# mLSTM of a two-layer diffusion backbone: masked attention over all keys replaced by 128-token blocks with carried states, and the projections interleaved with the blocks

## The chip, the core and the metric

The kernel runs on one core of a Trainium2 chip. A core has TensorE (PE, matmuls, with PEld loading its weights), VectorE (DVE), ScalarE (ACT), GpSimd (POOL) and SyncE (SP), each with an instruction queue of its own that it works through in order. ScalarE, GpSimd and SyncE also issue DMA transfers from their queues. The metric is the device time of one execution in microseconds.

## The reference, cut to what matters

512 latent tokens and 256 context tokens, width 1024, go through two layers. Layer 0 is a mixer and a convolutional FFN; layer 1 is latent attention and an FFN. The change touches layer 0's mixer only. It projects the normed tokens to a gated convolution branch (`a`, `g`), to `q`, `k`, `v`, an output gate `o` and 16 gate columns, runs a 31-tap depthwise convolution on the first branch and an mLSTM in both directions on the rest, and multiplies both, side by side, by `w_out`:

```python
def step(carry, inp):
...
    c_mat, n_vec, m = carry
    b = jnp.cumsum(lf, axis=-1)
    log_d = jnp.where(lower, b[..., :, None] - b[..., None, :] + li[..., None, :], -jnp.inf)
    log_inter = b + m[..., None]
    m_row = jnp.maximum(log_inter, jnp.max(log_d, axis=-1))
    s = jnp.einsum('bhid,bhjd->bhij', qj, kj) * jnp.exp(log_d - m_row[..., None])
    inter = jnp.exp(log_inter - m_row)
    num = jnp.einsum('bhij,bhjv->bhiv', s, vj) + inter[..., None] * jnp.einsum('bhvd,bhid->bhiv', c_mat, qj)
    den = jnp.sum(s, axis=-1) + inter * jnp.einsum('bhd,bhid->bhi', n_vec, qj)
    h = num / jnp.maximum(jnp.abs(den), jnp.exp(-m_row))[..., None]
...
h_ctx_seq, st_f, st_b = scans(ctx, zero, zero)
h_lat_seq, _, _ = scans(lat, st_f, st_b)
...
u = jax.nn.silu(_layer_norm(_dwconv(a * jax.nn.sigmoid(g), conv_w, conv_b), ln_g, ln_b))
hm = _rms(h_seq) * head_gain * jax.nn.sigmoid(o)
y = jnp.concatenate([u, hm], axis=-1) @ w_out
```

4 heads, keys of 64, values of 128. The forward scan runs over the context and then the latent tokens, the backward scan over each of them reversed. What chunk length is used does not change the result, and neither does computing the whole as masked attention over all earlier keys.

## The kernel before, in words

Tokens lie on the free axis in six tiles of 128 (0 to 3 latent, 4 and 5 context), channels on the partitions. A projection (`proj`, L160) splits weights and activations into two `fp32r` halves and sums three products: weight halves `wh` (ScalarE, L156) and `wl` (a subtraction, on GpSimd in the mixer, L157), the raw load `wr` on SP. An output tile of 128 channels is 48 matmuls of 384 columns. Each engine works in the order in which the scheduler lays its instructions; weights are given a priority that lifts them ahead of their place in the program.

`mixer0` (L507) goes through these steps:
- load, modulation, and the four GLU tiles (`pa`, `pg`, L569 to L593). Each gives an `up`, and 30 taps on VectorE (`conv_taps`, L560) that are taken up in small portions by `step` while later projections run.
- gate columns (`gwh`/`gwl`, `pgt`), then `gates` (L699): the log gates, prefix sums and running maxima (scans, L736 to L743), and for each of six blocks a row of decays `rr`, written to DRAM as table `rd` from ScalarE's queue (L782 to L787).
- `v` (L681) and `q`/`k` (L667), both kept as two `fp32r` halves; the output gate `so`, a tanh (L614).
- `mlstm` (L842 on): 12 units of a head and a pair of query tiles. For each unit the scores over all keys (`pqk`, three products each), broadcast loads of `rd` rows into `rf` and `rb`, masks on GpSimd, exponents, products with the scores and row sums on VectorE, transposes of the result (`pt`, split to `pth`/`ptl`), and the product with `v` (`phm`). A string `PAT0` sets in which order a unit's parts, the layer norm of the conv branch (`layer_norm`, L791, generator `L`), the rest of the ada modulations (`ada_pe`, L290, `U`, with weight loads `wa` through the `wr` buffers) and the `early` part of `w_out` (`pea`, `E`) stand.
- the product with `w_out` (`pab`, L632 to L649), residual, and the row sums for the next norm; then the FFN.

## Time and profile before

| | us |
|---|---|
| median of 3 runs (lowest, highest) | 1813.59 (1813.35, 1816.11) |
| the profiled execution | 1809.91 |
| its span | 1807.8 |
| TensorE busy in the span | 1722.2 (95%), 9614 instructions |
| TensorE weight loads | 1547.6 (86%) |
| VectorE busy | 1185.6 (66%), 1957 instructions |
| ScalarE busy | 707.5 (39%) |
| GpSimd busy | 251.4 (14%) |
| chain that ended last, by engine | PE 79%, DVE 11%, DMA 3%, ACT 3% |

The mean granted clock of TensorE is 0.957 of full speed. The two FFNs and layer 1 take the larger part of the span, from 485 us on. The mixer of layer 0 lies between 64 us (the end of the loads and of the first GLU tile) and 485 us: projections and conv taps to 254, the mLSTM with the layer norm to 416, `w_out` to 485. Row names: `out<-in` gives the tiles, a line of a helper (L103, L106, L109, L112) stands for any instruction that goes through it, and `<-` behind idle time names what ended it.

### The profile page before, as it was taken

The numbers are of one execution on the slowest core, as the hardware profiler recorded it, in microseconds if no ns is written. First come the engines' busy times: TensorE is split into PE (matmuls) and PEld (weight loads), VectorE is DVE, ScalarE is ACT, GpSimd is POOL, SyncE is SP. The second block draws the span as 40 slices with busy tenths as digits, with TensorE's granted clock in tenths as the row PEclk, the third lists the DMA queues.
The fourth block names the chain that finished last, engine by engine and source line by source line (L and its number), as shares of the span: only waits on it lengthen the run. The fifth ranks groups of instructions, "written<-read, shape, count | busy, mean of one in ns | idle before, by whom it ended". The sixth has DMA issues, their size and how long they took to land.

```text
span 1807.8 us, 24942 instructions
## 1 busy us (share of the span) xinstructions
PE 1722.2 (95%) x9614; PEld 1547.6 (86%) x9614; DVE 1185.6 (66%) x1957; ACT 707.5 (39%) x1352; POOL 251.4 (14%) x346
## 2 busy tenths in 40 slices
PE   6969887999999999999999999899999899999998
PEld 3968875669899999999999879899988788888887
DVE  4798987768694646364334487778788854444453
ACT  4212236642342121212222345787776442332232
POOL 2324223314300000000000111233140200000000
PEclk8989997779999999999999999999999899999999
DMA  9311135546252436263121241101110133333322
GB/s 345 103 37 47 47 114 170 172 150 184 77 151 82 140 99 194 70 198 92 61 59 59 80 111 53 39 13 36 34 44 24 36 94 101 98 94 97 102 90 73
DMA packets 201638, 174.78 MB, mean 97 GB/s; under 512 B 9288, under 2 KB 175606, under 8 KB 201520
## 3 DMA queue, kind: packets, MB, share of 16 engines
q1 hardware_dynamic: 198848, 169.60, 30.7%
q0 software_dynamic: 1216, 3.34, 0.5%
q8 instruction: 76, 1.25, 0.3%
q10 hardware_dynamic: 1456, 0.25, 0.1%
q14 instruction: 42, 0.34, 0.1%
HBM read 167.83 MB, written 5.33 MB: 96 GB/s over the span
## 4 chain that ended last, share of the span: by engine, by line
PE 79%; DVE 11%; DMA 3%; ACT 3%; issue 2%; POOL 1%; SPq 0%; POOLq 0%; ACTq 0%; DVEq 0%
PE pfo L103 16%; PE pfg L103 16%; PE pfv L103 16%; DVE acc L564 6%; PE psc L103 3%; PE pab L103 3%; PE ppv L103 2%; PE pt L1354 2%; PE pmo L103 2%; PE puq L103 2%; PE pukv L103 2%; PE pf L103 2%; PE pqk L103 1%; PE pcq L103 1%; PE phm L103 1%
## 5 line engine op out<-in xcount | busy, mean ns | idle before, releaser
L106 ACT ACTIVATE wh<-wr 128x1024 fp32r<-128x1024 f32 (+3 forms) x205 | 204.5, 999 | 608.6 <-PE pfo L103 220.4
L157 DVE TENSOR_TENSOR wl<-wr,wh 128x1024 fp32r<-128x1024 f32 (+3 forms) x171 | 195.6, 1146 | 195.4 <-ACT wh L106 191.4
L103 PE MATMUL pfo<-hh,wh 128*128 128x384 f32 (+2 forms) x528 | 167.2, 356 | 0.0
L103 PE MATMUL pfo<-hl,wh 128*128 128x384 f32 (+2 forms) x528 | 166.5, 354 | 0.0
L103 PE MATMUL pfo<-hh,wl 128*128 128x384 f32 (+2 forms) x528 | 166.2, 354 | 0.0
L112 DVE SCALAR_TENSOR_TENSOR xr<-pfo,mods,xr 128x512 f32<-128x512 f32 (+1 forms) x128 | 83.7, 664 | 105.5 <-PE pfo L103 104.9
L103 PE MATMUL pfg<-fh,wh 128*128 128x384 f32 (+1 forms) x504 | 151.9, 355 | 0.0
L103 PE MATMUL pfg<-fl,wh 128*128 128x384 f32 (+1 forms) x504 | 151.4, 354 | 0.0
L103 PE MATMUL pfg<-fh,wl 128*128 128x384 f32 (+1 forms) x504 | 151.1, 353 | 0.0
L103 PE MATMUL pfv<-fh,wh 128*128 128x384 f32 (+1 forms) x504 | 150.6, 352 | 0.0
L103 PE MATMUL pfv<-fh,wl 128*128 128x384 f32 (+1 forms) x504 | 150.6, 352 | 0.0
L103 PE MATMUL pfv<-fl,wh 128*128 128x384 f32 (+1 forms) x504 | 150.6, 352 | 0.0
L564 DVE SCALAR_TENSOR_TENSOR acc<-up,par,acc 128x783 f32<-128x783 f32 x120 | 135.4, 1165 | 1.9 <-ACT acc L106 1.1
L157 POOL TENSOR_TENSOR wl<-wr,wh 128x1024 fp32r<-128x1024 f32 (+1 forms) x34 | 93.1, 2740 | 252.3 <-ACT wh L106 234.2
L112 DVE SCALAR_TENSOR_TENSOR ga<-gr,cc,ga 128x1024 f32<-128x1024 f32 (+1 forms) x84 | 99.7, 1215 | 24.4 <-DMA gr<-in_ada_w_dram 24.3
L235 POOL TENSOR_TENSOR ss<-ss,sq 128x256 f32<-128x256 f32 (+1 forms) x31 | 32.6, 1057 | 583.1 <-ACT sq L106 581.5
L109 DVE TENSOR_TENSOR ft<-ft,pfv 128x768 f32<-128x768 f32 (+1 forms) x42 | 34.4, 820 | 109.9 <-PE pfv L103 109.9
L103 PEld LDWEIGHTS pfo<-hl,wh 128*128 128x128 f32 x528 | 98.1, 189 | 8.8 <-issue 0.2
L103 PEld LDWEIGHTS pfo<-hh,wh 128*128 128x128 f32 x528 | 97.8, 189 | 9.0 <-ACT hh L106 0.4
L103 PEld LDWEIGHTS pfo<-hh,wl 128*128 128x128 f32 x528 | 97.9, 189 | 8.8
L103 PEld LDWEIGHTS pfg<-fl,wh 128*128 128x128 f32 x504 | 92.8, 189 | 6.5
L103 PEld LDWEIGHTS pfg<-fh,wh 128*128 128x128 f32 x504 | 92.6, 189 | 6.6
(410 smaller groups left out, 3929.4 us busy)
## 6 DMA issues: line engine op xcount, KB each, us to landing
wr<-in_ffn_w_in_dram SPq DMA_DIRECT2D x88, 512.0 KB
gr<-in_ada_w_dram SPq DMA_DIRECT2D x48, 512.0 KB
wr<-in_ffn_w_out_dram SPq DMA_DIRECT2D x32, 512.0 KB
wa<-in_ada_w_dram SPq DMA_DIRECT2D x24, 512.0 KB
wr<-in_ab_w_in_dram SPq DMA_DIRECT2D x20, 512.0 KB
wr<-in_ffn_w_out_dram SPq DMA_DIRECT2D x24, 384.0 KB
wa<-in_ada_w_dram SPq DMA_DIRECT2D x8, 1024.0 KB
gr<-in_ada_w_dram SPq DMA_DIRECT2D x16, 256.0 KB
```

The lines of the kernel that those rows point to most:

```text
L103: self.nc.tensor.matmul(out, lhsT=lhsT, rhs=rhs, start=start, stop=stop)
L106: self.nc.scalar.activation(out, in_, func, **kw)
L109: self.nc.vector.tensor_tensor(out, a, b, op=op)
L112: self.nc.vector.scalar_tensor_tensor(out, a, s, b, op0=op0, op1=op1, **kw)
L157: self.lo_eng.tensor_tensor(lo[:, :n], raw[:, :n], hi[:, :n].bitcast(F32), op=ALU.subtract)
L235: eng.tensor_tensor(self.ss[:, s:e], self.ss[:, s:e], sq[:, s:e], op=ALU.add)
L564: nc.vector.scalar_tensor_tensor(acc[:, :CONVO], up[:, k:k + CONVO], self.convw[:, 4 * k + ct:4 * k + ct + 1], acc[:, :CONVO], op0=ALU.mul ...
L1354: nc.tensor.transpose(pt[:, o:o + P], pe[:, (j + jj) * P:(j + jj + 1) * P], self.ident)
```

## The change

The blocks carry a state per head, `C` (64 by 128 values and, through a column of ones beside `v`, the normaliser: 129 columns). `update` transposes a block of `k`, weighs it with `wc`, multiplies it with `v1` and adds the decayed old state. Five backward states `cb` are computed ahead, in the order 5, 4, 3, 2, 1; the forward state `cf` goes on with each block. A block takes scores of its own 128 keys alone (`pst`), the exponents `ex` (from table `ad`, loaded on SP, masked on GpSimd), and the carried part `ib` (table `qd`, multiplied with `q` on GpSimd); `pn` sums both for each direction, its last column is `den`. All of these products are plain float32. No broadcast rows `rf`/`rb`, no halves of `q`, `k` or `v`, no transposed probabilities. `finish` norms two blocks and multiplies them into `so`.

```diff
+PAT0 = 'c' + 'mtttt' * 3 + 'c' + 'mttttt' * 2 + 'ctttt' + 'mttttt' + 'c' + 'omtttttt' * 4 + 'F' + 'mmallmall' * 6
+MH = 3
-EM = 2
+MLSTM = {"S": (2, 2), "M": (2, 2)}
...
             gg = self.gates(pgt, gsm, slot)
             next(gg)
-            vt = self.vproj(win, hs, slot)
-            self.qkproj(win, hs, qk := [])
+            q, k = self.qkproj(win, hs)
+            for _ in glu(1):
+                self.step(TAP)
+            v1 = self.vproj(win, hs)
             G = next(gg)
...
+            gens = {"c": [glu(2), glu(3)], "o": [gate_o()], "a": [mods()], "m": [cell], "l": [ln]}
+            for o in PAT0:
+                if o == "t":
+                    self.step(1)
+                elif o == "F":
+                    self.flush()
+                else:
+                    run(o)
...
+            for m in range(MH):
+                w = self.weights(wout, 0, 4, m * P, P)
+                pss.append(self.psum_even("pab"))
+                self.proj(pss[m], w, 0, ins, 4, both, last=False)
...
+        for i, r in enumerate((f, b)):
+            nc.scalar.dma_start(ad[i].rearrange("t h n -> h t n"), blocks(a)[r])
...
+        for i in range(2):
+            for h in range(4):
+                r = 32 * i + h
+                nc.scalar.dma_start(dd[i, h // 2, h % 2:h % 2 + 1], dec[r:r + 1])
+                nc.scalar.dma_start(qd[:, h % 2, i, h // 2:h // 2 + 1].rearrange("t o n -> o t n"), blocks(ir)[r:r + 1])
+        for i in range(2):
+            for h in range(4):
+                nc.scalar.dma_start(dcol[64 * (h % 2):64 * (h % 2) + 64, 2 * i + h // 2],
+                                    dd[i, h // 2, h % 2:h % 2 + 1].partition_broadcast(64))
...
+        def update(i, t, old, new):
+            ps = self.pt("M", "pu")
+            for pr in range(2):
+                nc.tensor.transpose(ps[:, pr * P:(pr + 1) * P], k[pr][:, bl(t)], self.ident)
+            kw = mp.tile([P, 4, 64], F32, tag="kw", bufs=1, name=self.name("kw"))
+            self.tt(kw, ps[:, :256].rearrange("p (h c) -> p h c", h=4),
+                    wc[:, t, i].unsqueeze(2).to_broadcast([P, 4, 64]), ALU.mult)
+            for pr, o in ((0, 512), (1, 0)):
+                self.mm(ps[:, o:o + W2], kw[:, 2 * pr:2 * pr + 2, :].rearrange("p h c -> p (h c)"), v1(pr, t), True, True)
...
+            ex = [mp.tile([P, 4, P], F32, tag="ex", bufs=3, name=self.name("ex")) for _ in range(2)]
...
+                for h in range(4):
+                    self.act(ex[i][:, h], ex[i][:, h], AF.Exp, bias=cc[:, t, i, h:h + 1])
+            ib = mp.tile([P, 2, 2, P], F32, tag="ib", bufs=2, name=self.name("ib"))
...
+                        if st is not None:
+                            self.mm(pn[:, o + b * VW:][:, :VW], ib[:, i, pr], st[:, b * VW:(b + 1) * VW], True, False)
+                        self.mm(pn[:, o + b * VW:][:, :VW], ex[i][:, 2 * pr + b], v1(pr, t)[:, b * VW:(b + 1) * VW], st is None, True)
```

In `PAT0`, `c` is half a GLU tile (2 and 3), `o` one output gate, `t` one conv tap, `m` one part of `mlstm` (an update, or a third of a block), `a` half of an ada modulation, `l` a piece of the layer norm, `F` what is left of the taps. The order of the projections becomes GLU0, gates, q/k, GLU1, v, and then this string; `early` is gone, and the upper half of three `w_out` tiles (`MH`) stands behind the mLSTM instead.

Three places show how the instructions move. The first is GpSimd's queue ahead of the weights of GLU1's second half: `wl_1036` is the low half of GLU1's first, `wl_1090` that of its second; `ex` and `ib` are the exponents and carried parts of the first two blocks. As changed:

```order
L165 TENSOR_TENSOR wl_1036<-wr_1034,wh_1035 128x1024
L982 AFFINE_SELECT ex_1655<-ex_1655 128x512
L982 AFFINE_SELECT ex_1656<-ex_1656 128x512
L982 AFFINE_SELECT ex_1985<-ex_1985 128x512
L745 MEMSET v_139_1151 128x6
...
L991 TENSOR_TENSOR ib_1673<-ib_1673,qk_845 128x2x128
L991 TENSOR_TENSOR ib_1673<-ib_1673,qk_973 128x2x128
L991 TENSOR_TENSOR ib_2003<-ib_2003,qk_845 128x2x128
L991 TENSOR_TENSOR ib_2003<-ib_2003,qk_973 128x2x128
L165 TENSOR_TENSOR wl_1090<-wr_1088,wh_1089 128x1024
```

Three masks and four products of the mLSTM stand between the two weight halves. Before, GLU1 had both of its halves early, and the gate scans' initial values alone stood between later ones:

```order
L157 TENSOR_TENSOR wl_1242<-wr_1240,wh_1241 128x1024
L728 MEMSET mk_1115 36x768
...
L157 TENSOR_TENSOR wl_1292<-wr_1290,wh_1291 128x1024
L733 MEMSET m_1119 36x768
L734 MEMSET pf_1120 36x768
L157 TENSOR_TENSOR wl_1374<-wr_1372,wh_1373 128x1024
L772 MEMSET rr_1667 36x768
L157 TENSOR_TENSOR wl_1446<-wr_1444,wh_1445 128x1024
```

The second place is ScalarE's queue at the same point, as changed; `fg` and `z` are gate rows, `wh_1089` is the high half of GLU1's second weights. The 16 issues to `dd` and `qd` alternate, two rows of them stand here:

```order
L831 DMA ad<-fg_705 4x6x128 x2
L111 ACT_TABLE_LOAD
L111 ACTIVATE dec<-dec 36x6
L111 ACTIVATE qk_973<-pqk_924 128x768
L111 ACTIVATE z_716<-z_716 36x768
L849 DMA dd<-dec 1x6
L850 DMA qd<-z_716 6x1x128
...
L853 DMA dcol<-dd 64x6 x8
L111 ACTIVATE qk_1030<-pqk_981 128x768
L111 ACTIVATE wh_1089<-wr_1088 128x1024
```

Before, the table's issues came between the projections of `so`; here the weights behind the gates' last activation follow at once:

```order
L106 ACTIVATE fg_1097<-pgt_1037 36x768
L106 ACTIVATE e_1103<-fg_1097 36x768
L106 ACTIVATE e_1103<-e_1103 36x768
L106 ACT_TABLE_LOAD
L106 ACTIVATE z_1108<-w_1106 36x768
L106 ACTIVATE wh_1291<-wr_1290 128x1024
L106 ACTIVATE wh_1373<-wr_1372 128x1024
L106 ACTIVATE wh_1445<-wr_1444 128x1024
```

So the 26 issues, each of which waits for its gate row, stand ahead of a weight half that GLU1 needs.

The third place is TensorE in the last part of the mLSTM: `pada` the ada products, `pu` an update, `pst` the scores of a block, `pn` its sums. As changed:

```order
L108 MATMUL pada_2464<-wa_2467,cc_107 32x512 x2
L108 MATMUL pr_2486<-ss,sel 6x128 x5
L936 MATMUL pu_2516<-ident,qk_910 128x128
L936 MATMUL pu_2516<-ident,qk_1030 128x128
L108 MATMUL pada_2464<-wa_2473,cc_107 32x512 x2
L108 MATMUL pu_2516<-v_139_1151,kw_2519 128x258
L108 MATMUL pst_2581<-qk_845,qk_910 128x128 x2
L108 MATMUL pst_2581<-qk_973,qk_1030 128x128 x2
L108 MATMUL pada_2464<-wa_2475,cc_107 32x512 x2
L108 MATMUL pu_2516<-v_141_1153,kw_2519 128x258
L108 MATMUL pn_2590<-cf,ib_2576 128x129
L108 MATMUL pn_2590<-v_139_1151,ex_2558 128x129
```

Before, at the like place, a unit's products and transposes stood between them:

```order
L103 MATMUL pac_2867<-selq,arow_2802 128x2 x4
L103 MATMUL pr_2826<-hsq_2578,sel 6x128 x4
L103 MATMUL pada_2873<-wa_2874,cc_107 32x512 x2
L103 MATMUL pada_2873<-wa_2943,cc_107 32x512 x2
L103 MATMUL phm_2949<-pth_2858,vh_1344 128x256
L103 MATMUL phm_2949<-ptl_2859,vh_1344 128x256
L103 MATMUL phm_2949<-pth_2858,vl_1345 128x256
```

The ada products now stand between one block's update and the next block's scores and sums.

## Rows read from the trace of the kernel before

**Rows 1.** windows of the span: us, busy of each engine (instructions), granted clock, DMA share, GB/s

```profile
64.00:254.00 190.00, 167.47 (x882) 158.09 (x880) 181.21 (x201) 40.65 (x58) 60.29 (x34) 0.94 0.17 48
254.00:416.00 162.00, 144.06 (x716) 98.69 (x716) 116.73 (x370) 91.13 (x181) 41.38 (x71) 0.78 0.55 173
...
485.00:1808.00 1323.00, 1298.59 (x7376) 1193.28 (x7376) 806.34 (x1228) 530.26 (x1034) 99.29 (x192) 0.98 0.28 83
```

**Rows 2.** chain of waits, 64 to 300 us: start, length, what

```profile
75.23 3.07 DVE acc L564
...
92.92 15.48 DVE acc L564 x14
...
132.04 9.52 PE pgt L103 x44
141.57 4.54 PE pv L103 x20
...
162.79 3.94 DVE pf L736
...
175.87 0.95 DVE c L109
...
252.08 1.56 DMA rd<-rr
253.79 2.88 DMA rf<-rd
```

**Rows 3.** tile `acc`, the conv taps: duration ns min/median/max, first and last start

```profile
L564 DVE SCALAR_TENSOR_TENSOR acc<-up,par,acc x120: 1012/1022/3185, 71.0 to 248.8; 128x783 f32<-128x783 f32 x120
```

**Rows 4.** groups of instructions by shape, VectorE, 254 to 416 us: busy, mean ns

```profile
L109 DVE TENSOR_TENSOR ptl<-pt,pth 128x512 fp32r<-128x512 f32 x28 | 18.7, 677 | 6.7 <-ACT pth L106 6.7
...
L112 DVE SCALAR_TENSOR_TENSOR rf<-rb,dr,rf 128x128 f32<-128x128 f32 x20 | 7.2, 360 | 9.2 <-ACT rf L106 9.0
...
L112 DVE SCALAR_TENSOR_TENSOR dr<-den,dr 128x2 f32<-128x2 f32 x24 | 5.9, 244 | 0.1
...
L112 DVE SCALAR_TENSOR_TENSOR acc<-th,acc 128x768 f32<-128x768 f32 x4 | 3.8, 945 | 0.0
```

**Rows 5.** the same view, ScalarE, 64 to 416 us

```profile
L106 ACT ACTIVATE wh<-wr 128x1024 fp32r<-128x1024 f32 x17 | 18.0, 1057 | 74.2 <-PE pqk L103 14.9 <-PE pv L103 14.7 <-issue 9.3
...
L106 ACT ACTIVATE rf<-rf,acol 128x128 f32<-128x128 f32 x8 | 3.2, 394 | 4.8 <-POOL rf L873 4.8
```

**Rows 6.** tile `pm`, the one product of plain float32 over wide columns

```profile
L103 PE MATMUL pm<-s,ones x4: 379/486/697, 272.9 to 274.1; 128*128 128x512 f32 x2, 128*128 128x256 f32 x2
```

**Rows 7.** waits, 64 to 254 us: who for whom, total us, times, longest

```profile
ACT so L106 <- DMA rd<-rr: 12.4, 1, 12.4
...
PE pgt L103 <- DVE gwl L109: 10.9, 1, 10.9
```

**Rows 8.** chain of waits, 250 to 490 us

```profile
341.37 4.96 DMA wa<-in_ada_w_dram
...
416.75 33.83 PE pab L103 x192
...
484.87 1.22 PE pf L103 x2
```

**Rows 9.** tile `rd`, one kind of DMA issue on ScalarE's queue: ns min/median/max

```profile
L787 ACTq DMA_DIRECT2D rd<-rr x6: 247/250/253, 216.7 to 252.1; - x6
```

**Rows 10.** groups by shape, GpSimd, 64 to 485 us

```profile
L873 POOL TENSOR_SCALAR_AFFINE_SELECT rf<-rf 128x128 f32<-128x128 f32 x24 | 8.8, 371 | 43.0 <-DMA rf<-rd 42.5 <-PE pada L103 0.4
...
L235 POOL TENSOR_TENSOR ss<-ss,sq 128x256 f32<-128x256 f32 x6 | 5.8, 968 | 0.0
```

**Rows 11.** timeline of GpSimd, 74 to 97 us: start, length, what

```profile
74.25 3.21 POOL L157 TENSOR_TENSOR wl<-wr,wh 128x1024 fp32r<-128x1024 f32 x1 [5.00 <-ACT wh L106]
```

**Rows 12.** DMA issues, 254 to 416 us, the ada weights

```profile
wa<-in_ada_w_dram SPq DMA_DIRECT2D x21, 512.0 KB
```

More of the change, by code (lines that the diff above doesn't have):

```diff
@@ L467, in load_x @@
         nc = self.nc
-        xs = [self.xp.tile([P, T], F32, tag="x", name=f"x{k}") for k in range(KD)]
+        xs = [self.xtile(f"x{k}") for k in range(KD)]
         def src(t, c0, c1):
@@ L568, in mixer0, with glu @@
             accs = []
-            for ct in range(4):
+            def glu(ct):
                 if ct == 0:
@@ new lines, in mixer0 @@
+            hm = []
+            for h in range(4):
+                hi = ob.tile([P, T], F32R, name=self.name("hmh"))
+                gain = self.hgain[:, h:h + 1]
+                self.act(hi, so[:, h], AF.Copy, scale=gain)
+                lo = ob.tile([P, T], F32R, name=self.name("hml"))
+                self.stt(lo, so[:, h], gain, hi.bitcast(F32), ALU.mult, ALU.subtract)
+                hm.append((hi, lo))
+            xs = []
+            for k in range(KD):
+                xs.append(self.xtile(f"xr{k}"))
@@ L665, in gate_weights, with qkproj @@
         return gwh, gwl
-    def qkproj(self, win, hs, qk):
-        qk.extend([None] * 4)
+    def qkproj(self, win, hs):
+        out = [None] * 4
         for m in (0, 2, 1, 3):
@@ L687, in vproj, with gates @@
                               c == 0, c == 3, 2 * c)
[L688 to L699 removed]
+            self.step(TAP)
+        for t in range(NT):
+            for pr in range(2):
+                src = pst[t // 2][:, t % 2 * 512 + pr * 256:][:, :256].rearrange("p (b v) -> p b v", b=2)
+                self.act(v1(pr, t).rearrange("p (b v) -> p b v", b=2)[:, :, :P], src)
+        return v1
+    def gates(self, pgt, gsm, slot):
         nc = self.nc
@@ L743, in gates @@
         nc.vector.tensor_tensor_scan(m[b, rl], lf[b, rl], li[b, rl], m[b, LAT:LAT + 1], op0=ALU.add, op1=ALU.max)
-        tot = self.small.tile([R, 6], F32, tag="tot", name="tot")
-        pv = pf.rearrange("p (b n) -> p b n", n=P)
-        nc.vector.tensor_copy(tot[f], pv[f, :, P - 1])
-        nc.vector.tensor_copy(tot[b], pv[b, :, 0])
-        c = row("c")
+        tot, ml, mp = cells("tot"), cells("ml"), cells("mp")
+        for x, y in ((tot, pf), (ml, m)):
+            nc.vector.tensor_copy(x[f], blocks(y)[f, :, P - 1])
+            nc.vector.tensor_copy(x[b], blocks(y)[b, :, 0])
@@ L792, in layer_norm @@
+        yield cc, wc, em, ad, qd, dcol
+    def layer_norm(self, accs, uh, slot, pslot):
         nc = self.nc
@@ new lines, in mlstm, with finish @@
+        order = ORDER[1]
+        for i in range(5):
+            update(1, order[i], cb[:, i - 1] if i else None, cb[:, i])
+            yield
+        rows = [((0, [[0, 4], [1, P]], -1)), ((1, [[0, 4], [-1, P]], 1))]
+        done = []
+        def finish(t0, hu, ss):
+            r = self.small.tile([P, 8], F32, tag="hr", bufs=2, name=self.name("hr"))
+            self.rsqrt(r, ss, P, [P, 8])
+            yield
+            ps = self.pt("M", "pht")
+            for j in range(2):
+                for h in range(4):
+                    x = hu[j][:, h]
+                    self.act(x, x, AF.Copy, scale=r[:, 4 * j + h:4 * j + h + 1])
+                    o = j * 512 + h * P
+                    nc.tensor.transpose(ps[:, o:o + P], x, self.ident)
+            y = so[:, :, t0 * P:(t0 + 2) * P].rearrange("p h (j n) -> p h j n", n=P)
+            for j in range(2):
+                self.stt(y[:, :, j], y[:, :, j], 1.0, ps[:, j * 512:(j + 1) * 512].rearrange("p (h n) -> p h n", h=4),
+                         ALU.add, ALU.mult)
+            yield
@@ L1001, in ffn @@
+        yield from finish(*done.pop())
     def ffn(self, layer, xs, segs, nsegs, tail=None, gemv=()):
```

443 lines of the change are left out of this document (185 added, 258 removed).

## The prediction

> **What bounds the kernel now.** I read the busy shares by stretch first [rows 1]. The change touches 64 to 485 us; behind it lie 1323 us in which no instruction changes its work, so the question is when the first FFN matmul can start. It starts at 484.87 now. In 64 to 254 us VectorE is busy for 181.2 of 190 us and TensorE for 167.5. In 254 to 416 us neither is full: TensorE 144.1 of 162 at a granted clock of 0.78, VectorE 116.7. Next I read the chain of waits [rows 2]. Up to 254 us it runs almost wholly through the conv taps (15.48 us for 14 of them in one piece), the gate scans and the table `rd`; TensorE's pieces in it are short. So the first stretch is VectorE's, and what matters is how much VectorE work the change takes away, and where VectorE stands idle afterwards. The taps are 120 instructions, median 1.022 us, longest 3.185 [rows 3]; with the step to the next I price one at 1.04.
>
> **VectorE's work.** From the first `up` to the last work on `so`, the instructions that the order lists for the change, priced by like shapes, come to 234 us:
> - 30 taps of conv0 (31.2) and the gate chain (23.4, where the trace shows 13.1 us from the first scan to `c`, and 0.95 for each full row [rows 2]): 54.6.
> - `up` and 30 taps of conv1: 32.4.
> - five backward updates and `up`: 6.3. A `kw` of 256 columns and four state updates of 129 cost at most 0.36 each and at least 0.24 [rows 4]; I take 0.3 for the latter, nearer the wider end.
> - 60 taps (62.4) with blocks 0 and 1, `up` and the sums for LN: 78.1. A block is two products of 512 (0.68 each), six small ones (0.24 or less), four of 128 (0.36) and an update [rows 4]: 5.6 us.
> - blocks 2 to 5, LN (about 18 passes of up to 0.95 [rows 4]), the three finishes and the ada sums: 63.
>
> The two stretches of before hold 298 us. What goes is the score products, the `ptl` and `vl`/`ql` splits, the `rf`/`rb` products and the `rd` table. ScalarE gets 8 exponents, 4 scalings and 4 squares per block at 0.39 [rows 5]: about 40 us in all, beside 41 of 190 and 91 of 162 us busy [rows 1], so hidden, unless its queue blocks (below). TensorE: two plain float32 products of 512 and 256 columns took from 272.9 to 274.1 plus 0.38, that is 1.6 us or 2.1 ns a column [rows 6]. The change has 10 updates of 516 columns, 24 scores of 128 and 88 products of 129: 19,600 columns, 41 us, and 44 transposes; in place of nearly all the products of a stage with 144 busy. So TensorE is not the bound, with 20 us more if all ran at half clock.
>
> **Where the time goes, stage by stage.** If VectorE ran through, the FFN would start near 400. It won't, because of three queues.
>
> *A, 64 to the start of conv1's taps.* The gate weights no longer stand behind 14 taps on VectorE (now TensorE waits 10.9 us for `gwl` [rows 7] and starts `pgt` at 132.04); they come at about 72. `pgt` takes 9.5 [rows 2], to 82; four q/k projections at 8.46 (192 matmuls took 33.83 [rows 8]) to 116; the first half of GLU1 to 124. Its second half needs a split on ScalarE (1.06 [rows 5]) and on GpSimd, and both queues hold gate work first. VectorE's 54.6 us from 72 put the last gate row at about 121, with two or three GpSimd hits at 126. Then ScalarE's exponent (at most 0.95) and 24 of its 26 DMA issues at 0.25 [rows 9] give 133, or 134.5 with a landing of 1.56 before `dcol` [rows 2]. GpSimd has the three masks and four `ib` products in front: the `ib` wait for `qd`, issued by 131, to land and be read back, 1.56 and 2.88 [rows 2], then four at 0.97 [rows 10], then the split `wl` 3.21 [rows 11]: 142.5, or some 5 us less if block 0's gates come early. GLU1's weights are there at 137 to 143: TensorE stands 13 to 19 us, and VectorE, out of taps, somewhat longer. GLU1 ends at 146 to 152.
>
> *B, to conv2's taps.* The v projection is 144 matmuls at 0.227 (20 took 4.54 [rows 2]), 33 us, to 179 to 185; conv1's taps end at about 184 to 190. PSUM changes hands, 12 evacuations, then GLU2 (17) with the backward updates (7 to 9): conv2 starts at 208 to 214, I take 211. VectorE idles for some 20 us here.
>
> *C, to the last tap.* 78 us of VectorE, and the `wl` splits of GLU3 and o beside it. A tap beside a GpSimd split took 3.07 [rows 2] for 1.05: 2 us each. Six of them are 12. The last tap ends at 301.
>
> The Trainium skill ("GPSIMD Engine Reference", § 1. Specifications) says that GpSimd shares its SBUF interfaces with VectorE, and that VectorE instructions in a 2-port mode or with two SBUF inputs contend. It speaks of no form of the GpSimd operation, so the 12 masks would slow taps and LN passes as the splits do; masks of 128 columns took 0.37 [rows 10], so my estimate for 512 is 1.5 us each, and at two thirds of that lost the sum by it comes out up to 11 us later. No row here shows a mask beside a tap. The sum itself keeps the masks at nothing: three of the twelve run in stage A while VectorE has no taps left, and most others in the tail, beside a VectorE that waits in between.
>
> *D, the tail* (blocks 2 to 5, LN, ada). 63 us of VectorE. The mLSTM stretch of before, with the same kind of chain through all engines, took 162 us for 116.7 us of VectorE work [rows 1]. At the same ratio: 87 us, to 388. Bounds: 63 if nothing waits, 118 and more if the ada loads set the pace (first rival).
>
> *E, to the FFN.* Before, from the first `pab` (416.75) to 484.87: 68.1 us [rows 8]. The two early u-halves (48 matmuls, 8.5) come back into it, and the new u-halves start about 2 us ahead of the last `so`: 74.6. FFN at 463.
>
> **Sum:** 463 against 484.9, 22 us earlier. The profiled execution took 1809.9 (span 1807.8), so **1788**. The median of the three runs stands 3.7 us above it. A difference within 0.2% (3.6 us) is about what a measurement of this kernel can't tell from none.
>
> **Rivals.**
> 1. *The ada loads set the tail, slower.* All three remaining ada blocks, 24 loads of 512 KB, now fall into a tail of about 87 us; before, 21 of them lay in 162 us at a DMA share of 0.55 [rows 1, 12]. They go through the weight buffers, on SP's queue behind the `ex` and `ib` loads, which wait for buffers. `pada` stands in TensorE's order between the blocks, so one late load holds the block behind it. Such a wait took 4.96 us in the chain [rows 8]. The tail has 46 us to spare over its 63 before the gain is gone: decided at 9 loads that wait in full. At 12 the tail is 123 us: 301 + 123 + 74.6 = 499, and **1824**. For it: same buffers, half the time. Against: loads are issued up to three ahead, and waits overlap with VectorE's own work. Chance 0.18.
> 2. *The gate queues don't hold GLU1, much faster.* If GpSimd and ScalarE reach GLU1's weights in time, VectorE has taps all along: 72 + 171.4 (A to C) + 16 for eight hits = 259; with D and E as above the FFN starts at 421: **1746**. With a tail free of waits too, 1722. For it: TensorE is 9.5 + 34 us ahead of its need. Against: the order of the queues leaves no other way than through the gate rows. Chance 0.18.
> 3. *Even.* The gain is eaten by holds that I rate too low (the tail at 105 to 112 us): within 0.2%, **1810**. Chance 0.06.
>
> **How the numbers follow.** The forecast's own case, with A to D at other values within their bounds (tail 75 to 104, hold 6 us either way), gives 1770 to 1806, chance 0.58. Rival 2 adds 0.18 on the fast side, so faster 0.76, same 0.06, slower 0.18. The range for 8 in 10 takes in rival 2's first value and most of rival 1: 1742 to 1822.
>
> **What would show it.** Right: `pgt` starts near 72; TensorE stands more than 10 us before GLU1's second half, with ScalarE's DMA issues or GpSimd's `ib` named as releaser; conv2's first tap near 211; last tap near 301; first `pab` near 386; first FFN matmul near 463, and from there on the spans are equal. Wrong: no hold in front of GLU1 and taps in one run (rival 2); waits for `wa` in the chain of the tail adding up to more than 46 us (rival 1); or any shift behind the first FFN matmul, for which I have no term. A taps' median far from 1.02 would say that GpSimd or the new layout of buffers costs VectorE more than the splits alone.

## The result and the profile after

The changed kernel takes **1792.43 us** (median of 4 executions, 1790.63 to 1794.76), the kernel before 1813.88 beside it (4 executions, 1813.35 to 1816.11): a ratio of **0.988, 95% interval 0.9863 to 0.9897**. Forecast were 1788.0 and faster by over 0.2%; the time lies 4.4 us above the point and inside the range. The profiled execution took 1791.37 us, its span 1789.6. Every start and end below is read from one profiled execution of each kernel.

The first view is again the busy time by stretch. The columns are those of [rows 1]; the stretches end at the forecast's own marks as they came out (last tap, first `pab`, first `pf`).

```profile
64.00:124.00 60.00, 53.54 (x291) 52.14 (x291) 56.29 (x68) 16.99 (x23) 16.53 (x15) 0.91 0.21 58
124.00:150.00 26.00, 13.04 (x54) 12.21 (x53) 3.28 (x3) 3.65 (x4) 12.49 (x13) 0.67 0.29 83
150.00:215.00 65.00, 62.91 (x305) 53.43 (x304) 46.91 (x50) 19.58 (x45) 18.38 (x13) 0.97 0.18 50
215.00:304.00 89.00, 76.99 (x406) 63.94 (x405) 77.74 (x100) 20.15 (x55) 16.56 (x11) 0.88 0.28 88
304.00:391.00 87.00, 63.41 (x324) 40.01 (x323) 60.63 (x154) 39.50 (x113) 32.48 (x31) 0.76 0.58 184
391.00:470.00 79.00, 76.89 (x436) 73.30 (x436) 40.03 (x57) 21.48 (x32) 32.52 (x21) 0.95 0.31 90
470.00:1789.00 1319.00, 1294.36 (x7376) 1189.56 (x7376) 807.12 (x1229) 530.67 (x1035) 99.15 (x192) 0.99 0.28 84
```

Two stretches stand out. From 124 to 150 us TensorE is busy for 13.0 of 26 us and VectorE for 3.3: this is the hold in front of GLU1's second half. From 304 to 391 us the busiest engine, TensorE, works for 63.4 of 87 us: the tail. Everywhere else TensorE is busy for 86% of the time or more, also in the two stretches that the prediction gave to VectorE (64 to 124 and 215 to 304 us, where VectorE is busy for 94% and 87%). The last line answers to the last of [rows 1] with the same 7376 matmuls.

The chain of waits shows what the hold is made of (start, length, what; `ACTq` is a DMA issue on ScalarE's queue, L849 `dd`, L850 `qd`, L853 `dcol`):

```profile
120.66 0.68 ACT z L111
121.36 0.79 ACTq L850
...
122.19 0.42 ACTq L849
...
130.41 0.52 ACTq L853
...
133.11 0.61 ACTq L853
133.76 2.38 DMA dcol<-dd
136.14 1.39 POOL ib L991 x2
...
137.69 2.38 POOL wl L165
...
140.12 10.66 PE pg L108 x44
150.78 14.24 PE pv L108 x61
```

The issues run one behind the other from 120.4 to 135.8 us, and only the first `dd` (0.23 us) is as short as the 0.25 us of [rows 9]. Apart from one activation (`z`) ScalarE does nothing else meanwhile, GpSimd's `ib` wait for what the issues send, and the split `wl` of GLU1's weights stands behind the `ib`. Both queues come to GLU1's weights at the same time: the last `ib` ends at 137.5 us, and the high half `wh` that the split needs at 137.6. The waits have the same seen from the engines that stand (total us, times, longest; the last line lies in the tail):

```profile
PE pg L108 <- ACT wh L111: 12.2, 1, 12.2
...
DVE up L117 <- ACT sg L111: 25.0, 1, 25.0
...
PE pada L108 <- DMA wa<-in_ada_w_dram: 8.4, 6, 2.7
```

The taps, tile `acc`, cost what they cost before [rows 3]:

```profile
L571 DVE SCALAR_TENSOR_TENSOR acc<-up,par,acc x120: 1002/1034/3177, 71.6 to 303.4; 128x783 f32<-128x783 f32 x120
```

Last the chain of the tail and of `w_out`:

```profile
309.54 4.69 DMA ib<-qd
...
330.02 4.27 DMA wa<-in_ada_w_dram
...
339.40 4.28 DMA wa<-in_ada_w_dram
...
345.75 6.09 DMA ib<-qd
...
391.25 35.66 PE pab L108 x192
...
470.71 1.22 PE pf L108 x2
```

In the tail the chain goes through every engine and both queues in pieces of a few microseconds; waits for ada loads (`wa`) are two of 4.27 and 4.28 us, and one of 4.55 at 281.63, before this stretch, far from the 46 that rival 1 needed.

**Where the gain is.** The FFN's first matmul `pf` starts at 470.7 instead of 484.9 [rows 8]: 14.2 us of the 18.2 by which the spans differ. The other 4.0 us lie behind it, where no instruction changed its work: 2.7 of them in the first 110 us of the first FFN, 1.2 more by the first products of layer 1. Windows of equal distance from each kernel's first `pf`, before and then after:

```profile
484.90:544.90 60.00, 60.00 (x330) 56.99 (x331) 54.94 (x82) 23.82 (x31) 0.00 (x0) 0.95 0.44 130
544.90:604.90 60.00, 60.00 (x350) 60.00 (x349) 37.20 (x45) 12.59 (x13) 0.00 (x0) 0.97 0.35 106
```

```profile
470.70:530.70 60.00, 59.99 (x336) 57.04 (x337) 54.72 (x81) 23.76 (x31) 0.00 (x0) 0.97 0.46 143
530.70:590.70 60.00, 60.00 (x359) 60.00 (x358) 39.82 (x48) 12.58 (x13) 0.00 (x0) 1.00 0.38 114
```

TensorE is busy throughout in all four, but gets through 336 matmuls instead of 330 and 359 instead of 350, at a granted clock of 0.97 and 1.00 instead of 0.95 and 0.97. This part goes with the clock of that execution, not with a step of the change, and below it varies between 1318.7 and 1325.2 us from kernel to kernel. So of the 21.4 us between the medians, 14.2 are traced to the changed stages. The experiments are therefore compared by the first `pf`, and the totals stand beside it.

### The profile page after: what moved, and what is told of

Read it like the earlier page. It is cut to its first block, busy times and chain, and to the rows that moved or that the text cites. A ratio compares the mean times of both kernels' runs of the same rounds, so it can differ in the third digit from the quotient of the medians.

```text
span 1789.6 us, 24209 instructions
## 1 busy us (share of the span) xinstructions
PE 1688.4 (94%) x9432; PEld 1518.9 (85%) x9432; DVE 1119.6 (63%) x1745; ACT 677.7 (38%) x1359; POOL 247.5 (14%) x333
## 4 chain that ended last, share of the span: by engine, by line
PE 82%; DVE 8%; DMA 3%; ACT 2%; issue 2%; POOL 1%; ACTq 1%; SPq 0%; DVEq 0%; POOLq 0%
PE pfo L108 17%; PE pfg L108 16%; PE pfv L108 16%; PE pab L108 4%; DVE acc L571 3%; PE psc L108 3%; PE ppv L108 2%; PE pt L1390 2%; PE pf L108 2%; PE puq L108 2%; PE pv L108 2%; PE pmo L108 2%; PE pukv L108 2%; DMA wa<-in_ada_w_dram 1%; PE pg L108 1%
## 5 line engine op out<-in xcount | busy, mean ns | idle before, releaser
L108 PE MATMUL pfv<-fh,wh 128*128 128x384 f32 (+1 forms) x504 | 150.6, 352 | 0.0
L108 PE MATMUL pfv<-fl,wh 128*128 128x384 f32 (+1 forms) x504 | 150.6, 352 | 0.0
L108 PE MATMUL pfv<-fh,wl 128*128 128x384 f32 (+1 forms) x504 | 150.6, 352 | 0.0
L571 DVE SCALAR_TENSOR_TENSOR acc<-up,par,acc 128x783 f32<-128x783 f32 x120 | 140.2, 1175 | 4.6 <-ACT acc L111 2.2
L165 POOL TENSOR_TENSOR wl<-wr,wh 128x1024 fp32r<-128x1024 f32 (+1 forms) x35 | 80.6, 2307 | 221.1 <-ACT wh L111 221.1
```

The lines of the kernel that those rows point to most:

```text
L108: self.nc.tensor.matmul(out, lhsT=lhsT, rhs=rhs, start=start, stop=stop)
L165: self.lo_eng.tensor_tensor(lo[:, :n], raw[:, :n], hi[:, :n].bitcast(F32), op=ALU.subtract)
L571: nc.vector.scalar_tensor_tensor(acc[:, :CONVO], up[:, k:k + CONVO], self.convw[:, 4 * k + ct:4 * k + ct + 1], acc[:, :CONVO], op0=ALU.mul ...
```

## The experiments

The theory after the result: (1) the hold comes from whose queue GLU1's weights stand in, and costs its full length at `pf`; (2) from there to the last tap VectorE's work sets the pace; (3) the tail is a chain with a length of its own, which starts at the last tap. Rivals: the ada loads set the tail; TensorE sets (2) and (3). All times in the table are us; each is the first start in the profiled execution, for `o`'s end and the last tap the start of the last; "behind" is the span less the first `pf`.

| kernel | v | o's end | last tap | first `pab` | first `pf` | behind |
|---|---|---|---|---|---|---|
| before | 141.4 | 251.0 | 248.8 | 416.7 | 484.9 | 1322.9 |
| changed | 150.6 | 277.6 | 303.4 | 391.3 | 470.7 | 1318.9 |
| e1 gate_prio | 144.0 | 273.9 | 299.6 | 386.1 | 466.0 | 1324.1 |
| e2 fewer_taps | 151.3 | 278.2 | 275.4 | 387.8 | 467.0 | 1320.3 |
| e3 ada_early | 152.6 | 332.3 | 303.3 | 402.1 | 481.4 | 1324.2 |
| e4 ex_four | 150.0 | 275.5 | 299.4 | 392.5 | 471.8 | 1319.0 |
| e5 gate_prio_qk | 135.4 | 270.8 | 297.2 | 384.8 | 464.2 | 1318.7 |
| e6 no_ada_loads | 149.7 | 276.6 | 296.0 | 383.9 | 463.1 | 1322.1 |
| e7 blocks_last | 151.2 | 259.0 | 283.5 | 412.6 | 492.1 | 1325.1 |
| e8 pn_twice | 153.7 | 283.2 | 297.1 | 396.1 | 475.8 | 1325.2 |
| e9 ten_issues | 141.5 | 268.5 | 294.3 | 379.0 | 458.2 | 1322.3 |
| e10 ten_and_prio | 136.3 | 269.8 | 295.6 | 381.6 | 461.2 | 1324.1 |
| e11 no_gemv | 152.8 | 279.8 | 305.8 | 390.4 | 470.6 | 1320.9 |
| e12 v_on_vector | 134.5 | 259.9 | 285.7 | 370.6 | 449.7 | 1322.4 |

Seven of these kernels (e2, e3, e4, e6, e7, e8, e11) change nothing that stands ahead of v, and v starts in them at 149.7 to 153.7 us. So a difference of 3 us or less from the changed kernel can't be told from none.

### The hold, first try: the weights' priority (e1)

```diff
-  self.proj(ps, self.weights(win, 0, KD, c0 + ct * P, P, 0 if ct == 1 else WPRIO), 0, hs, KD, both)
+  self.proj(ps, self.weights(win, 0, KD, c0 + ct * P, P, WPRIO + 300), 0, hs, KD, both)
...
-  w = self.weights(win, 2 * c, 2, 1536, 512)
+  w = self.weights(win, 2 * c, 2, 1536, 512, WPRIO + 300)
```

> The weights of GLU1's second half and of v get a higher priority, so that their splits stand ahead of the mLSTM's ib products on GpSimd and of most gate DMA issues on ScalarE; no instruction is added or dropped, TensorE's order is the same. Theory (TensorE stands from 124 to 140 us because these splits wait behind the gate queues, and VectorE runs out of taps for it): the hold of 16 us goes, the v projection starts near 133 instead of 150.6, conv2's first tap near 199 instead of 215, the first FFN matmul near 455 instead of 470.7, total 1775 to 1780. Rival (the hold is given back, since taps and blocks are paced by something later): under 5 us faster, 1788 to 1793.

Measured: 1791.43 us, ratio 0.9854 (0.9817 to 0.9891); first `pf` 466.0. v starts only 6.6 us earlier. Its chain, from what ends last before v:

```profile
139.44 3.62 DMA dcol<-dd
...
143.10 0.82 ACT qk L111
```

TensorE's own timeline names the same releaser:

```profile
143.96 0.79 PE L108 MATMUL pv<-wh,hh 128*128 128x512 f32 x1 [9.92 <-ACT qk L111]
```

GLU1 runs through to 134 us, then TensorE stands for 9.9 us, until 144. The weights have left the queue; the evacuation of the last q/k product has not. It stands behind the issues on ScalarE and holds the PSUM that v needs. The hold has a second leg.

### The second leg too (e5)

```diff
+  with self.tc.high_priority(offset=WPRIO + 300):
       self.act(out[m], ps[:, :T], AF.Copy, scale=1.0 if m < 2 else 0.125)
```

> As the first run with higher priority for GLU1's and v's weight splits, and ScalarE's evacuations of q and k moved ahead of the gate DMA issues as well, since in that run v still waited to 144 us for a q/k accumulator that ScalarE empties behind the dcol issues. Theory (that was the second leg of the same hold): v starts at 133 to 136, the first FFN matmul at 452 to 458 instead of 470.7 (466.0 with the first leg alone), total 1772 to 1782 at the FFN clock of the changed kernel. Rival (a third wait takes its place, or the stretch after it gives the time back): first FFN matmul at 463 to 468.

Measured: 1785.76 us, ratio 0.9837 (0.9804 to 0.987); first `pf` 464.2. v starts at 135.4, 15.2 us earlier than in the changed kernel, and only 6.5 of them are left at `pf`, as the rival had it. TensorE still stands for 6.7 us inside v, until 147.9. The chain says who is late now:

```profile
143.88 2.24 DMA dcol<-dd
146.12 1.05 ACT wh L111
147.17 0.71 ACT sg L111
```

`sg`, the sigmoid that conv1's taps wait for, and v's next `wh` stand behind the same issues. Each leg that is lifted leaves the next instruction of ScalarE's queue there.

### The cause taken away: eight issues for 24 (e9)

The table of decays goes out in two transfers (`dd`), `qd` in four (each direction and parity of the head), `dcol` comes back in two:

```diff
-            for h in range(4):
-                r = 32 * i + h
-                nc.scalar.dma_start(dd[i, h // 2, h % 2:h % 2 + 1], dec[r:r + 1])
-                nc.scalar.dma_start(qd[:, h % 2, i, h // 2:h // 2 + 1].rearrange("t o n -> o t n"), blocks(ir)[r:r + 1])
+            nc.scalar.dma_start(dd[i].rearrange("r b t -> (r b) t"), dec[32 * i:32 * i + 4])
+            for b2 in range(2):
+                nc.scalar.dma_start(qd[:, b2, i].rearrange("t r n -> r t n"), blocks(ir)[32 * i + b2:32 * i + 4:2])
...
+        for b2 in range(2):
+            nc.scalar.dma_start(dcol[64 * b2:64 * b2 + 64].rearrange("p (i r) t -> p i r t", i=2),
+                                dd[:, :, b2].unsqueeze(0).partition_broadcast(64))
```

> The 24 gate DMAs of ScalarE's queue that carry dd, qd and dcol become 8 of the same bytes (one dd per direction, one qd per direction and head parity, two dcol); nothing else. In the changed kernel these 24 took from 120.4 to 135.9 us, 0.42 to 0.67 us each, not the 0.25 of the forecast. Theory (that queue time is what GLU1's weights and the last q/k evacuation wait for): the hold ends 7 to 10 us earlier, v starts at 141 to 144 instead of 150.6, first FFN matmul at 461 to 465 instead of 470.7. Rival (GpSimd's wait for the landed qd sets it, the number of issues does not matter): v at 148 or later, first FFN matmul within 3 us of 470.7.

Measured: 1783.4 us, ratio 0.9848 (0.9827 to 0.9869); v at 141.5 and first `pf` at 458.2, 9.1 and 12.5 us ahead of the changed kernel and ahead of the theory's 461 to 465. TensorE stands for 3.6 us in front of GLU1's second half instead of 13.0, and in its chain neither an issue nor `ib` is left. An issue of two rows (`qd`) or of four (`dcol`) takes about as long as one of one row did, 0.67 and 0.61 (tiles `qd` and `dcol` of e9, ns min/median/max):

```profile
L849 ACTq DMA_DIRECT2D qd<-z x4: 597/614/762, 122.1 to 124.7; - x4
...
L851 ACTq DMA_DIRECT2D dcol<-dd x2: 622/648/675, 125.4 to 126.1; - x2
```

But the edit had a second effect, which its text does not show: GpSimd's queue has another order. Its timeline, of the changed kernel and then of e9 (in brackets the idle time ahead and what ended it):

```profile
134.76 2.77 POOL L991 TENSOR_TENSOR ib<-ib,qk 128x256 f32<-128x256 f32 x4 [8.06 <-DMA ib<-qd]
137.69 7.03 POOL L165 TENSOR_TENSOR wl<-wr,wh 128x1024 fp32r<-128x1024 f32 x3 [0.17 <-ACT wh L111]
```

```profile
128.62 4.69 POOL L165 TENSOR_TENSOR wl<-wr,wh 128x1024 fp32r<-128x1024 f32 x2 [1.15 <-ACT wh L111]
134.07 2.81 POOL L989 TENSOR_TENSOR ib<-ib,qk 128x256 f32<-128x256 f32 x4 [0.77 <-DMA ib<-qd]
```

The scheduler laid two weight splits ahead of the `ib` here. ScalarE's `wh` comes some 9 us sooner, as the theory has it, but the `ib` end at 136.9, only 0.6 us sooner. So 16 fewer issues, with the order on GpSimd that came with them, move the FFN by 12.5 us, and theory (1) holds in that the hold goes with those two queues. What fewer issues alone are worth, with the `ib` still in front, is not shown; the rival, GpSimd's wait for the landed `qd`, is not excluded as a second leg.

### Both (e10), and v's halves on VectorE (e12)

e10 is e9 with the priorities of e1 and e5.

> The fewer gate DMAs together with the earlier weight splits and q/k evacuations of the run e5. In e5 v began at 135.4, but GLU1's tanh, behind the dcol issues on ScalarE, only at 147, so that conv1's taps and with them the first update began hardly earlier, and 8 of the 15 us were given back. Theory: with the short queue the tanh comes by 136 to 140, v runs through, conv2's first tap is 12 to 16 us earlier than in the changed kernel (199 to 203), first FFN matmul 455 to 459, total 1771 to 1780. Rival (the stretch behind gives it back again): first FFN matmul 462 to 466, total 1780 to 1788.

Measured: 1786.49 us, ratio 0.9859 (0.9837 to 0.9881); first `pf` 461.2, 3.0 us later than e9 alone. v starts at 136.3, but its second weights are late, and TensorE stands for 5.2 us in front of them:

```profile
142.90 4.30 POOL ib L990 x3
147.20 3.04 POOL wl L165
150.28 9.85 PE pv L108 x31
```

On GpSimd the split has stood behind the `ib` all along; now that v comes early, TensorE meets it. e12 gives these splits to VectorE:

```diff
         for c in range(4):
+            self.lo_eng = nc.vector
             w = self.weights(win, 2 * c, 2, 1536, 512, WPRIO + 300)
+            self.lo_eng = nc.gpsimd
```

> The kernel of the run before last with fewer issues and both priorities, and v's low halves formed on VectorE instead of GpSimd. In that kernel TensorE still stands from 142 to 150 us for v's second weights, which lie on GpSimd behind the four products of the gates (they wait for the transfer of qd), while VectorE does nothing there. Theory (the hold is a matter of whose queue the weights stand in): v runs through from about 135 us, conv1's first taps come 5 to 8 us sooner, the first product of the FFN at 452 to 457 us (458.2 and 461.2 in the two kernels it is made from), total 1772 to 1780. Rival (given back behind: VectorE has some 4 us more to do before the taps, and the stretches behind take up the rest): first product of the FFN at 458 to 462 us, total 1780 to 1788.

(Wrong of e10 was that VectorE does nothing there: the taps of conv1 had begun at 140.15. And TensorE stood from 145.1, not from 142.) Measured: **1775.9 us, ratio 0.9808 (0.9784 to 0.9833)**, the fastest of all; first `pf` at 449.7, ahead of the 452 to 457 that the theory gave. GLU1 and v are one piece:

```profile
117.82 8.45 PE pa L108 x48
126.27 8.44 PE pg L108 x48
134.71 33.48 PE pv L108 x144
```

v is 16.1 us earlier than in the changed kernel, o's end 17.7, `pab` 20.7, `pf` 21.0. Nothing is given back. How long TensorE stands between GLU1's first half and the end of v, and the first `pf`, go together through all six kernels: 13.0 us in the changed kernel, 9.9 in e1, 6.7 in e5, 5.2 in e10, 3.6 in e9 and none in e12, with `pf` at 470.7, 466.0, 464.2, 461.2, 458.2 and 449.7. In each of them `pf` gains at least what TensorE stands less, so the hold does cost its full length; where the 5 us beyond v's 16.1 come from is not. They are not a lighter VectorE: the four splits take it 6.0 us, and its 120 taps 140.9 us after 140.2 in the changed kernel (147.2 in e10, where more of them stand beside a GpSimd split).

With no hold the time is still far from rival 2's 1746. The windows of e12 from the first `pgt` to conv2's first tap, from there to o's end, and to the end of the last tap say why:

```profile
74.00:197.30 123.30, 121.23 (x636) 111.29 (x637) 107.60 (x115) 36.37 (x64) 39.51 (x31) 0.99 0.25 65
197.30:260.00 62.70, 56.72 (x324) 54.62 (x323) 61.29 (x71) 13.18 (x32) 14.21 (x7) 0.95 0.16 45
260.00:286.70 26.70, 20.69 (x90) 9.77 (x88) 16.93 (x31) 6.96 (x23) 2.65 (x4) 0.74 0.57 192
```

Up to conv2's first tap TensorE is full, with 121.2 of 123.3 us: the projections say when `up` and the taps can begin. From there to o's end VectorE is full, with 61.3 of 62.7. Behind it neither is. The changed kernel has the same in its last two stretches, from conv2's first tap to o's end and to the end of the last tap:

```profile
215.00:278.00 63.00, 57.06 (x327) 54.93 (x326) 61.54 (x71) 13.22 (x33) 13.92 (x7) 0.95 0.16 45
278.00:304.40 26.40, 20.33 (x84) 9.41 (x83) 16.60 (x30) 6.94 (x23) 2.64 (x4) 0.72 0.59 191
```

### VectorE's share: 15 taps fewer (e2)

```diff
-                for k in range(1, CW):
+                for k in range(1, CW if ct < 3 else CW - 15):
```

> Leaves out 15 of the 30 VectorE taps of the last conv tile. In the stretch from conv2's first tap to the last tap VectorE is busy 78 and TensorE 77 of 89 us. Theory (VectorE's order sets that stretch): the last tap ends 13 to 16 us earlier, near 289, total 1776 to 1780. Rival (TensorE or the block chain sets it): 0 to 5 us earlier, total 1787 to 1793.

Measured: 1791.2 us, ratio 0.987 (0.9851 to 0.9889). Tile `acc`:

```profile
L571 DVE SCALAR_TENSOR_TENSOR acc<-up,par,acc x105: 1005/1034/3174, 72.4 to 275.4; 128x783 f32<-128x783 f32 x105
```

The last tap comes 28.0 us earlier, more than either side expected, and the first `pab` 3.5. Theory (3) falls in this form: the tail does not begin at the last tap. On theory (2) e2 says less than was meant. The 15 taps left out are those that start from 275.9 us on in the changed kernel, so o's end, at 277.6, could hardly move, and it did not (278.2). Up to there VectorE's order is borne out by busy time alone (61.5 of 63 us, TensorE 57.1); behind it the last taps are not what the kernel waits for.

### The tail: loads, buffers, products, sums (e6, e3, e4, e8, e11)

e6 leaves out 18 of the 24 remaining ada loads:

```diff
+                if k == 0 or layer:
-                raw = self.wp.tile([P, 1024], F32, tag="wr", name=self.name("wa"))
+                    raw = self.wp.tile([P, 1024], F32, tag="wr", name=self.name("wa"))
...
-                self.nc.sync.dma_start(rv, w[k * P:(k + 2) * P, c0:c0 + 512].rearrange("(k p) c -> p k c", p=P))
+                    self.nc.sync.dma_start(rv, w[k * P:(k + 2) * P, c0:c0 + 512].rearrange("(k p) c -> p k c", p=P))
```

> Leaves out 18 of the 24 loads of the ada blocks 2 to 4: each half loads its first tile and uses it four times; matmuls, issues of tables and everything else stay. Theory (TensorE waits in the tail for ada weights that can only be loaded three ahead; 13 us of such loads in the chain, plus tables held on the same queue): tail from the last tap to the first product with w_out 65 to 75 us instead of 87, total 1772 to 1782. Rival (the blocks' own chain of table, mask, exponent, products sets the tail and the loads lie beside it): tail 82 to 87, total 1788 to 1793.

Measured: 1790.52 us, ratio 0.9863 (0.9828 to 0.9898). First `pab` at 383.9, 7.4 us earlier. From the last tap (296.0) to it there are still 87.9 us, as in the changed kernel, but after e2 that mark does not bound the tail. From o's end it is 107.3 us instead of 113.7, so 6.4 of the 7.4 us lie there: half of the 13.1 us that the chain of the changed kernel waits for `wa` (4.55, 4.27 and 4.28). Rival 1's price, loads that set the whole tail, does not show.

e3 puts the ada halves between the output gates:

```diff
-PAT0 = 'c' + 'mtttt' * 3 + 'c' + 'mttttt' * 2 + 'ctttt' + 'mttttt' + 'c' + 'omtttttt' * 4 + 'F' + 'mmallmall' * 6
+PAT0 = 'c' + 'mtttt' * 3 + 'c' + 'mttttt' * 2 + 'ctttt' + 'mttttt' + 'c' + 'oamttatttt' * 4 + 'F' + 'mmllmll' * 6
```

> The six halves of the ada modulations are moved from the tail to between the last conv taps. Theory (the tail of 87 us holds 13 us of waits for wa in the chain and some 10 us of pada and pac): tail 65 to 74 us, the tap stretch up to 8 us longer, total 1778 to 1786. Rival (the tail is paced by the blocks' own chain of table load, mask, exponent, product; the ada waits lie beside it): tail 80 to 87 us, tap stretch 0 to 8 us longer, total 1790 to 1800.

Measured: 1798.23 us, ratio 0.9925 (0.9901 to 0.9949); the tail from o's end to `pab` shrinks from 114 to 70 us, but o ends at 332.3 instead of 277.6, since the loads take the same buffers as the weights of `o`: its chain there has four waits of 3.65 to 4.04 us for `wa` and two of 3.81 and 5.46 for `wr`. First `pf` 10.7 us later, in a profiled execution that took 1807.4 us; the median is 5.8 us above the changed kernel's.

e4 gives `ex` a fourth buffer, so that the next block's loads need not wait (`jk` is narrowed to make room):

```diff
-            ex = [mp.tile([P, 4, P], F32, tag="ex", bufs=3, name=self.name("ex")) for _ in range(2)]
+            ex = [mp.tile([P, 4, P], F32, tag="ex", bufs=4, name=self.name("ex")) for _ in range(2)]
```

> A fourth buffer for the exponent tiles (the squares that nobody reads are written in bfloat16 to make room). Theory (the table loads ex and ib come late because SP waits for a free ex buffer, 11 us of ib loads in the tail's chain): total 5 to 10 us faster, 1782 to 1787. Rival (another wait ends at the same time, wa or the previous block's products): under 3 us either way, 1789 to 1795.

Measured: 1798.66 us, ratio 0.9905 (0.9883 to 0.9927); first `pf` 471.8, in the fastest execution of the four (1793.34). From o's end to `pab` it takes 117.0 us instead of 113.7, although no wait for `ib<-qd` is left in its chain there, where the changed kernel has two (4.69 and 6.09 us). So those waits can go without the tail getting shorter: others take their place.

e8 does the 88 products `pn` twice:

```diff
+  for _ in range(2):
       if st is not None:
           self.mm(pn[:, o + b * VW:][:, :VW], ib[:, i, pr], st[:, b * VW:(b + 1) * VW], True, False)
       self.mm(pn[:, o + b * VW:][:, :VW], ex[i][:, 2 * pr + b], v1(pr, t)[:, b * VW:(b + 1) * VW], st is None, True)
```

> Each of the 88 plain float32 products pn is done twice with the same result, 24 us more of TensorE at 0.27 us each. Theory (TensorE has room between the waits of the tail, and is nearly full in the tap stretch): two blocks' share, 7 us, shows in the tap stretch and less than half of the 17 us in the tail, total 8 to 15 us slower, 1800 to 1807. Rival (every TensorE us counts): 20 to 26 us slower, 1812 to 1819. Other rival (none counts): within 4 us.

Measured: 1799.98 us, ratio 0.9919 (0.989 to 0.9947). The groups of instructions give `pn` 39.2 us in the changed kernel and 67.2 here, 28 more, and `pf` comes 5.1 later, of which 3.1 are there at v already. That TensorE has room beside the blocks follows only in part: the granted clock from 64 to 470 us is 0.92 here and 0.87 there, and TensorE's busy time over this stretch rises by 7.3 us only (354.06 after 346.78), so shorter instructions gave much of it back. From o's end to `pab` the clock is 0.89 instead of 0.75, and the stretch takes 112.9 us after 113.7. What the products would have cost at one and the same clock can't be read from it.

e11 leaves out 12 of the 16 steps on VectorE of another ada modulation, which fall into the same time:

```diff
-            for k in range(KD):
+            for k in range(KD if layer else 2):
```

> Leaves out 12 of the 16 steps of ada modulation 5 on VectorE (a load gr of 256 KB and two products each), which the order lays into the tail and behind it. The tail takes 88 us with and without the waits for the ada loads wa. Theory (in the tail VectorE's own queue, with gr loads that it waits for in order, holds the blocks): first product with w_out 8 to 15 us earlier, near 380, total 1776 to 1784. Rival (the blocks' own chain of table, exponent, product and state sets the tail): first product with w_out within 4 us of 391, total 1787 to 1793.

Measured: 1793.24 us, ratio 0.9895 (0.9873 to 0.9917); `pab` and `pf` within 1 us of the changed kernel.

From o's end to the first `pab` the changed kernel takes 113.7 us, and five kernels that change nothing there (e1, e5, e9, e10, e12) 110.5 to 114.0. e2, e8 and e11 lie in this band or 1 us below it (109.6, 112.9, 110.6), e6 3 us below (107.3), e4 3 us above (117.0). Only moving the work itself changes it much: e3 (69.8, with o's end 55 us later) and e7.

### Without the interleaving (e7)

```diff
-PAT0 = 'c' + 'mtttt' * 3 + 'c' + 'mttttt' * 2 + 'ctttt' + 'mttttt' + 'c' + 'omtttttt' * 4 + 'F' + 'mmallmall' * 6
+PAT0 = 'ccttttccotttttttt' + 'otttttttt' * 3 + 'F' + 'mmmmm' + 'mmallmall' * 6
```

> Same instructions, other order: GLU2, GLU3 and the output gates first, with the conv taps, and all updates and blocks behind them. Theory (in the tap stretch both VectorE and TensorE are nearly full, so what the blocks use there is mostly gaps; in the tail they run at their own chain's pace of some 15 us a block): tap stretch 10 to 20 us shorter, tail 30 to 45 us longer, total 1805 to 1822. Rival (interleaving only moves work about): total 1788 to 1796.

Measured: 1818.75 us, ratio **1.0024 (1.0008 to 1.0041)**: no faster than the kernel before. Its windows up to the last tap and from there:

```profile
215.00:284.00 69.00, 59.29 (x301) 48.40 (x300) 65.54 (x72) 9.82 (x13) 7.95 (x3) 0.90 0.28 92
284.00:413.00 129.00, 86.16 (x417) 56.43 (x416) 77.02 (x192) 50.51 (x158) 39.16 (x39) 0.70 0.44 133
```

o ends 18.6 us earlier, but updates and blocks then run behind the taps for 129 us, with layer norm and ada, at TensorE 86 and VectorE 77. The first `pf` comes 21.4 us later than in the changed kernel: this is what putting the blocks between the projections is worth. The blocks by themselves are quicker than the masked attention all the same. From the last tap to the first `pab` e7 takes 129.1 us and the kernel before 167.9, both with the rest of ada and most of the layer norm in it. These 38.8 us are used up because the last tap comes 34.7 us later (283.5 after 248.8, with the hold still in front of GLU1), and from `pab` to `pf` it takes 79.5 us instead of 68.2, most of it because the early part of `w_out` is gone.

## Why the prediction was right, and where it was not

**A, the gates: right sum, two wrong terms.** `pgt` starts at 72.1 (72). The step "24 of its 26 DMA issues at 0.25" failed: they take 15.4 us, not 6 (`dd` 0.42, `qd` 0.67, `dcol` 0.61). The row of [rows 9] is an issue of another shape; shape is not the whole of it, since the first `dd`, with no issue directly ahead of it, took 0.23. Against that the gate rows were ready at 120.3, not 126. By luck the two cancel: weights at 140.1 (137 to 143), TensorE stands 13 us (13 to 19). The legs that e1 and e5 laid bare (`qk`, `sg`, v's `wh` behind the same issues) were missing. That these two queues are the cause is shown by e9 and e12; how the hold divides between ScalarE's issues and GpSimd's `ib` is not.

**B.** v ends at 182.3 (179 to 185), conv2's first tap starts at 215.0 (211), 32.7 us behind it instead of 29. The waits in the chain there were not tried.

**C: right number, by luck in part.** The last tap ends at 304.4 (301), 89.4 us behind conv2's first (90). The bound was right up to o's end, where VectorE is busy for 61.5 of 63 us. But the 12 us for six hits were not: three taps stood beside a split (2.46, 3.04 and 3.18 us), and they are inside VectorE's 78.1 busy us. What fills the sum instead is 11 us of idle VectorE, nearly 10 of them behind o's end, for which there was no term. "TensorE is not the bound" holds for this stretch (57.1 of 63 us) and fails ahead of conv2's first tap, where the projections lie (e12). The price of the new products was low as well: they took 63 us (`pn` 39.2, `pu` 16.5, `pst` 7.6 in the groups of instructions), not the 41 of the estimate from `pm` [rows 6], and near the 61 that it gave for half clock. Each is two records, and one of 129 columns is 0.445 us, not 0.27; in e8, at a granted clock of 0.92 instead of 0.87, it is still 0.38. So columns alone do not price a narrow product.

**Rival 2** failed by the step "VectorE has taps all along". Its condition was met in e12, which took 1775.9, not 1746. VectorE's work was priced well: 185.8 us busy from 74 us to the end of the last tap, against 187.4. But TensorE needs 121.2 of the 123.3 us up to conv2's first tap, and VectorE stands for 10 us behind o's end, so the last tap ends at 286.7 instead of 259.

**D: right number, cause open.** 86.9 us (87), by the ratio of busy to length in the old mLSTM stretch. The prediction let it follow the last tap; e2 excludes that. Taking out loads gave 6 us of 113.7 from o's end (e6, against rival 1); taking out waits for `ex` (e4) or VectorE's ada sums (e11) did not shorten it clear of noise, and more products (e8) did not lengthen it. That the chain of blocks through all engines does is argued from the chain and from e7, not shown; nor was shortening one block's own chain tried.

**E: 79.4 us, not 74.6.** The upper halves of `w_out` started after the last `so` instead of 2 us ahead of it, and 192 `pab` took 35.66 us, not the 33.83 of [rows 8]; the 8.5 us for the early halves were right. 68.1 + 8.5 + 1.8 is 78.4; about 1 us is left unexplained.

**Sum.** The FFN starts 8 us later than forecast (4 by B, 5 by E, 1 back in C), and 4 us come back behind it by the granted clock, for which there was no term: 1791.4 against 1788.0. The step "from there on the spans are equal" failed by those 4 us, a sign of being wrong that the prediction had named. That the total came this near is in part luck.

**The masks.** Taps beside two of them, in the timelines of VectorE and of GpSimd:

```profile
248.45 1.32 DVE L571 SCALAR_TENSOR_TENSOR acc<-up,par,acc 128x783 f32<-128x783 f32 x1
249.81 1.28 DVE L571 SCALAR_TENSOR_TENSOR acc<-up,par,acc 128x783 f32<-128x783 f32 x1
```

```profile
247.57 2.70 POOL L982 TENSOR_SCALAR_AFFINE_SELECT ex<-ex 128x512 f32<-128x512 f32 x2
```

A tap beside a mask loses about 0.3 us, where one beside a split takes up to 3.18. Five taps meet masks, three of them in stage A (1.28 us each from 123.4 us on), where the prediction saw VectorE out of taps; together they lose 1.3 us. Passes of the layer norm beside masks were not looked at. For the taps the sum's nothing was nearer than 11 us. The Trainium skill ("GPSIMD Engine Reference", § 1. Specifications) is borne out in that they contend; the size depends on the form, on which that section is silent.

## What to carry to other kernels

A DMA issue is work of the queue that it stands in: count issues at the duration of their own shape, and ask what waits behind them; here 16 issues fewer, with the order on GpSimd that came with them, moved the FFN by 12.5 us, nearly the 14.2 of the whole rewrite. Compare the order of every queue after an edit that was meant to leave it alone. When one wait is lifted, look for the next instruction on the same queue before calling the theory wrong: e1 and e5 moved the FFN by 5 and 7 us, e10 by less than e9 alone, and only all legs together by 21. Bound a stretch by the busy time of each engine within it, after the hold is taken out, and cut it where the work changes: from the first `pgt` to o's end e12 has TensorE at 178 of 186 us, but its last third belongs to VectorE. Before you read an experiment, look where the instructions that it leaves out stood.
